# Independent column groups, a new hand-written order, and the rotation's halves exchanged by DMA

## The chip, the cores and the metric

The kernel is one program on one core of a Trainium2 chip. The metric is the time of one execution in device microseconds; three executions of the kernel before took 726.45 to 727.84 us, median 726.69. Five engines work in it beside the DMA engines: TensorE (PE in the profile, its weight loads PEld), VectorE (DVE), ScalarE (ACT), GpSimd (POOL) and SyncE (SP). Each engine runs its own list of instructions in order and waits for the others by semaphores.

## The reference, cut to what matters

Two layers over 256 tokens of width 1024, batch 1, all in float32:

```python
for layer in range(2):
    shift, scale, gate = split(mods[2 * layer], 3)          # mods = silu(c) @ ada_w + ada_b
    h = modulate(x, norm_mix[layer], shift, scale)          # RMS norm, then scale and shift
    if layer == 0:
        y = hgrn2_mixer(h, ...)                             # gated linear recurrence, 8 heads, chunks
    else:
        shared = nsa_shared_kv(modulate(x, kv_norm, ...))   # six projections: k and v, three branches
        y = nsa_mixer(h, ..., shared, cos, sin)             # sparse attention, 16 heads, 4 kv heads
    x = x + gate * y
    h = modulate(x, norm_ffn[layer], *mods[2 * layer + 1][:2])
    x = x + gate2 * swiglu(h, ffn_w_in[layer], ffn_w_out[layer])
```

In the second mixer the keys of two branches and the queries are normalised per head and then rotated:

```python
def apply_rope(x, cos, sin):
    x1, x2 = jnp.split(x, 2, axis=-1)
    return jnp.concatenate([x1 * cs - x2 * sn, x2 * cs + x1 * sn], axis=-1)
```

The attention has a compressed branch (softmax over 15 compressed blocks), a selected and a window branch, whose three outputs are added with sigmoid gates.

## The kernel before, in words

**Products.** Activations lie with channels on the partitions and the 256 tokens along the free dimension. A float32 product is made of three products of float32r numbers: weights and activations are split into a high part (a rounded copy) and a low part (the rest), and high·high, high·low and low·high are summed in PSUM (`mm3`, L531 to L533; `gemm_wide`, L543 and L544, takes high·[high low] in one matmul of 512 columns and low·high in one of 256). The high part of a weight is an ACT copy (L321), the low part a DVE subtraction (L325), two halves of 1024 columns for each 1 MB of weights.

**Weights.** `SCHED` is the list of all 1 MB weight tiles in the order of their use. SP loads them (L298) into a ring of four buffers; `process` splits the next one, or hands it to the code that uses it raw.

**Orders.** A scheduling framework puts the traced instructions in order on each engine: a list by priority, which is the order of tracing, moved by offsets (`PRI`, `first`), with an instruction eligible when those that it depends on are done in the framework's own reckoning. `after` adds an edge between two instructions of one engine. Two matmuls into one PSUM tile count as dependent, whichever partitions they write. The strings in `ORDER` give the order of tracing within the two mixers:

- first mixer (`"hgrn"`): `D`n decays of heads (logs, cumulated products; DVE and ACT), `S`n scores, `V`n values and the squares for their norm, `T`n the end of the values (scale, transpose), `i`n and `g`n products with weight tiles, `G` and `H` gates, `o`n the output product. A token with `+` is put into a generator, `between`; `S1/4` takes four steps of it after each of 12 groups of score matmuls; `x` runs what is left of it. i and g have 16 steps each, T has 2.
- second mixer (`"nsa"`): `q`n product for a quarter of the queries, their squares and rotation; `c` the two halves of the compression with raw weights; `K` the modulated input of the value projections, split; `G` gates; `n`n head norm of the queries of two `q` tokens; `w`n value projections; `x`n compressed softmax; `s`n scores of a pair of heads and their softmax; `v`n transposes and the product with the values; `a` one weight tile of a modulation that TensorE computes.

**Modulations on TensorE** (`ada_pe`, L427): with a left operand of 32 columns the array is used in four column groups. A row of four matmuls, one for each group, accumulates one slice of the input channels into four partition groups of one PSUM tile. s1 and g0 (traced in the first mixer), g2 and s3 (in the second) are of this kind.

**Values** (`attend_values`): for a pair of heads, the probabilities are transposed (ptt, L1561), copied to SBUF (PT; one of four by DVE, three by ACT) and multiplied with the values in two column groups, one for each head of the pair: five steps for each half, into one PSUM tile po (L1578).

**Rotation.** `raw_heads` copies a projection to hu and squares it. `rotate` exchanges the halves of 32 channels by four ACT copies between partition groups (us, L1240; us has two buffers), then DVE makes gain·u·cos (L1243), swap·us·sin (L1244) and their sum (L1245). `head_norm` sums the squares (hs, L1255), takes the inverse root on ACT and DVE, spreads it over the partitions (hb, L1264 and L1265) and multiplies (L1266, for queries also L1268). It is called for the two keys before the string begins, and by `n`.

**End.** `ffn` ends with eight chunks of the output product of 22 weight blocks each. `residual` adds gate times the product to x, for `gemm_wide` in two DVE steps (L796), and SP stores the chunk (L800).

Of the kernel before, what the change touches and what calls it, by code (L numbers as in the profile page):

```python
# [55 lines left out]
def _ada_g(l):  # L56
# [6 lines left out]

ORDER = {
    "hgrn": (
        "D0 k i0 +g0 +i1 +g1 S0/4 x c0 c1 V0 D1 i2 +i3 +g2 +T0 +g3 S1/4 x G0 V1 T1 o0 H o1 G1 o2 o3"
    ).split(),
    "hada": [1, 1, 2, 2, 3, 3, 4, 4, 7, 7, 8, 8],
    "f0": [7, 7, 8, 8, 9, 13, 15, 16, 16, 16, 21, 21, 22, 23, 25, 26, 28, 29, 31, 32],
    "nsa": (  # L70
        "q0 c1 c0 K G q1 n0 x0 w0 s0 q3 s1 q2 w1 s2 v0 v1 n1 s3 a s4 v2 a v3 a x1 s5 a a s6 v4 v6 s7 v5 a v7 a a a a a a"
    ).split(),
    "f1": [15, 16, 24, 29],
}
# [125 lines left out]
class K:  # L200
# [101 lines left out]
    def process(self):  # L302
        nc = self.nc
        n = self.n_proc
        kind, name, i = SCHED[n]
        if SCHED[n] in LATE:
            self.n_proc += 1
            return
        self.issue(n + 1)
        self.n_proc += 1  # L310
        t = self.raw.pop(n)
        if kind in ("lin", "half"):
            ws = []
            for h in range(1 if kind == "half" else 2):
                c = CH // 2
                u = t[:, h * c:h * c + c]
                self.n_half += 1
                pool = self.xp if self.xp is not None and self.n_half % XMOD < 2 else self.wp
                wh = pool.tile([P, c], F32R, tag="wh", name=f"wh{n}_{h}")
                wl = pool.tile([P, c], F32R, tag="wl", name=f"wl{n}_{h}")  # L320
                r = nc.scalar.copy(wh, u)  # L321
                if h and self.hold is not None:
                    self.after(r, self.hold)
                    self.hold = None
                r = nc.vector.tensor_tensor(wl, u, wh.bitcast(F32), op=ALU.subtract)  # L325
                if (name, i, h) in ROOTED:
                    self.after(r, self.last_dg)
                ws.append((wh, wl))
            self.ready.append((name, i, ws))
        elif kind == "raw":  # L330
            self.rawready[(name, i)] = (n, t)
            self.held.add(n)
        elif kind in ("pe_ss", "pe_g"):
            self.ada_pe(kind[3:], name, i, t)
        else:
            self.ada(kind, name, i, t)
        self.issue(n + RAW + 1)
# [78 lines left out]
    def ada_pe(self, kind, l, i, t):  # L416

        nc = self.nc
        ss = kind == "ss"
        q = 512 if ss else 256  # L420
        if i == 0:
            self.aps = self.pp.tile([P, 512], F32, tag="ada", bufs=1, name=f"adaps{kind}{l}")
        ks = [i] if ss else [2 * i, 2 * i + 1]
        last = i == (7 if ss else 3)
        for n, k in enumerate(ks):
            for j in range(4):
                nc.tensor.matmul(self.aps[32 * j:32 * j + 32, :q], lhsT=self.c32[:, k],  # L427
                                 rhs=t[:, n * D + j * q:n * D + (j + 1) * q], start=k == 0, stop=k == KD - 1,
                                 tile_position=(0, 32 * j))
        if not last:  # L430
            return
        m, A, bias = self.ada_tiles(l)
        nb = q // P
        sm = self.tp.tile([P, 512], F32, tag="junk", bufs=1, name="adasm")
        nc.scalar.copy(sm[:, :q], self.aps[:, :q])
        pt = self.pp.tile([P, 4, P], F32, tag="ada", bufs=1, name="adat")
        for b in range(nb):
            nc.tensor.transpose(pt[:, b, :], sm[:, b * P:(b + 1) * P], self.c("ident"))
        lo, hi = (0, 16) if ss else (16, 24)
        nc.vector.tensor_tensor(m[:, lo:hi].rearrange("p (j b) -> p j b", b=nb),  # L440
                                pt.rearrange("p b (j r) -> p j b r", r=32)[:, :, :nb, 0],
                                bias[:, lo:hi].rearrange("p (j b) -> p j b", b=nb), op=ALU.add)
        if ss:
            nc.vector.scalar_tensor_tensor(A, m[:, 8:16], 1.0, self.col(self.gain(l)), op0=ALU.add, op1=ALU.mult)
            self.mods[("A", l)] = A
            self.mods[("shift", l)] = m[:, 0:8]
        else:
            self.mods[("gate", l)] = m[:, 16:24]
# [367 lines left out]
    def hgrn(self):  # L816
# [3 lines left out]
        with self.tc.tile_pool(name="hg", bufs=1) as gp, self.tc.tile_pool(name="hg2", bufs=2) as g2:  # L820
# [112 lines left out]
            for t in ORDER["hgrn"]:  # L933
# [5 lines left out]
                elif t[0] == "S":  # L939
                    As.update(self.hgrn_scores((2 * n, 2 * n + 1), Xs, q3, g2, between, int(t[3:] or 0)))  # L940
                elif t[0] == "+":
                    between = chain(between, {"g": gate_steps, "o": out_steps, "i": value_steps, "T": end_steps}[t[1]](int(t[2])))
                elif t[0] == "x":
                    for _ in between:
                        pass
                elif t[0] == "i":
                    for _ in value_steps(n):
                        pass
                elif t[0] == "g":
                    if n < 2:  # L950
                        nc.scalar.copy(graw[:, n], gate_in(n))
                    else:
                        gin[n] = None
                elif t[0] == "c":
                    nc.scalar.copy(graw[:, n], gin[n])
                elif t[0] == "V":
                    ends[n] = (2 * n, 2 * n + 1), *self.hgrn_values((2 * n, 2 * n + 1), As, v[n], g2, q), g2, q
                elif t[0] == "T":
                    for _ in self.values_end(*ends[n]):
                        pass  # L960
                elif t[0] == "G":
                    gated(n)
                elif t[0] == "H":
                    late.extend(gate_act(m, gin[m], "X") for m in (2, 3))
                elif t[0] == "o":
                    for _ in out_steps(n):
                        pass
            self.end_residual(nxt)
            self.h = nxt

# [198 lines left out]
    def ffn(self, l):  # L1169
        nc = self.nc  # L1170
        with self.tc.tile_pool(name=f"ff{l}", bufs=1) as fp, self.tc.tile_pool(name=f"ft{l}", bufs=2) as tp, \
# [38 lines left out]
            for m in range(KD):  # L1210
# [5 lines left out]
                            tiles[nch * 16 + 8 * h + e] = t  # L1216
                    nch += 1
                ps = self.acc_tile(f"ffo{l}_{m}")
                self.gemm_wide(ps, [tiles.pop(m * NF + k) for k in range(NF)], lambda k: g[:, k])
                self.residual(ps[:, 0], m, gate, nxt, ps[:, 1])  # L1220
            self.end_residual(nxt)
            self.h = nxt

# [10 lines left out]
    def rotate(self, u, gain, swap, kr, name):  # L1234
# [2 lines left out]
        us = self.s2.tile([P, 2, S], F32, tag="us", bufs=2, name=f"us{name}")  # L1237
        for b in range(4):
            d, e = 32 * b, 32 * (b ^ 1)
            nc.scalar.copy(us[d:d + 32], u[e:e + 32])  # L1240
        cs = self.c("cos")[:, None, :].to_broadcast([P, 2, S])
        sn = self.c("sin")[:, None, :].to_broadcast([P, 2, S])
        nc.vector.scalar_tensor_tensor(kr, u, gain, cs, op0=ALU.mult, op1=ALU.mult)  # L1243
        nc.vector.scalar_tensor_tensor(us, us, swap, sn, op0=ALU.mult, op1=ALU.mult)  # L1244
        nc.vector.tensor_tensor(kr, kr, us, op=ALU.add)  # L1245

    def head_norm(self, pairs, kr, gain=None, kn=None):

        nc = self.nc
        ps = self.m_tile([P, S], "hs")  # L1250
# [6 lines left out]
        r = self.rsqrt(ps, [P, S], "hr")  # L1257
        rh, rl = (self.tp.tile([P, S], F32R, tag=f"hr{e}", bufs=1, name=f"hr{e}") for e in "yt")
        self.split(rh, rl, r)
        for i, (u, _) in enumerate(pairs):  # L1260
            pb = self.m_tile([P, 2, S], "hb")
            for m in range(2):
# [7 lines left out]
    def nsa(self):  # L1270
        nc = self.nc
        with self.tc.tile_pool(name="ns", bufs=1) as sp, self.tc.tile_pool(name="ns2", bufs=2) as s2, \
                ExitStack() as self.late:
            self.sp, self.s2 = sp, s2
            self.PC, self.Pt = {}, {}
            self.rsel = sp.tile([P, 4 * P], F32R, name="rsel")
            rsel = s2.tile([P, 2, S], F32, tag="hsq", bufs=2, name="rselr").rearrange("p a b -> p (a b)")
# [16 lines left out]
            with ExitStack() as early:  # L1294
# [20 lines left out]
                hq = self.full_pair(1, 2, xr, s2, QACT)  # L1315
                for br in range(2):
                    self.rotate(kk[br][0], self.col("k_norm", 1 + br), self.col("k_swap", 1 + br), KR[:, :, br], f"k{br}")
                self.head_norm(kk, [KR[:, :, br] for br in range(2)])
                for kind in range(2):
                    self.cmp_blocks(*dk[kind], kind, Dt[kind], sk)  # L1320
                self.QR = sp.tile([P, 8, S], F32, name="QR")
# [20 lines left out]
                for t in ORDER["nsa"]:  # L1342
                    n = int(t[1:] or 0)
                    if t[0] == "q":
                        query(n)
                    elif t[0] == "K":
                        hk.append(self.full_pair(0, "kv", xr, s2, KACT))
                        early.close()
# [201 lines left out]
    def attend_values(self, j):  # L1550
# [20 lines left out]
        for br in range(2):  # L1571
            for e, t in ((0, slice(0, S)), (1, slice(P, S))):
                steps.append((br, self.V[:, e, br, P * g:P * g + P].rearrange("p (h d) -> p h d", h=2),
                              slice(0, S) if e == 0 else slice(S, 384), t))
        for n, (br, w, r, t) in enumerate(steps):
            for half in range(2):
                rhs = r if br is None else PT[half, br][:, r]
                nc.tensor.matmul(po[64 * half:64 * half + 64, t], lhsT=w[:, half], rhs=rhs, start=n == 0,  # L1578
                                 stop=n == len(steps) - 1, tile_position=(0, 64 * half))
        self.split(self.O[0][:, j, :256], self.O[1][:, j, :256], po)  # L1580


# [117 lines left out]
```

## Time and profile before

| | us |
|---|---|
| median of 3 runs | 726.69 |
| the profiled execution | 726.5 |
| its span, first to last instruction | 724.7 |
| TensorE busy | 711.4 |
| VectorE busy | 578.6 |
| ScalarE busy | 433.7 |
| GpSimd busy | 0.4 |

Stages on TensorE, from the timeline: first mixer to about 170 us, first feed-forward to 359, keys and values of the second mixer from 359, its string of tokens from 385 to 510, output product to 537, second feed-forward to the end. The granted clock is 1.00 throughout.

How to read it: the span's 13.3 us without TensorE work lie at the start, at the end and in a few places between. Times in rows are microseconds from the span's start; `xN` is a count of instructions, a float32 matmul counts as two (two passes), a float32r one as one. An arrow `<-` at the end of a row names what the idle time before it waited for. A group row gives busy time, the mean duration in ns, and idle time before it. Matmuls overlap, so what one costs is read from start to start.

### The profile page before, as it was taken

The numbers are of one execution on the slowest core, as the hardware profiler recorded it, in microseconds if no ns is written. First come the engines' busy times: TensorE is split into PE (matmuls) and PEld (weight loads), VectorE is DVE, ScalarE is ACT, GpSimd is POOL, SyncE is SP. The second block draws the span as 40 slices with busy tenths as digits, with TensorE's granted clock in tenths as the row PEclk, the third lists the DMA queues.
The fourth block names the chain that finished last, engine by engine and source line by source line (L and its number), as shares of the span: only waits on it lengthen the run. The fifth ranks groups of instructions, "written<-read, shape, count | busy, mean of one in ns | idle before, by whom it ended". The sixth has DMA issues, their size and how long they took to land.

```text
span 724.7 us, 14519 instructions
## 1 busy us (share of the span) xinstructions
PE 711.4 (98%) x5821; PEld 626.3 (86%) x5821; DVE 578.6 (80%) x1177; ACT 433.7 (60%) x849; POOL 0.4 (0%) x5
## 2 busy tenths in 40 slices
PE   7999999999999999999998999999999999999997
PEld 4998788799999999988897996555999888888886
DVE  6997896589999889889598898677779878776651
ACT  5669877567635454544379776558657656564430
POOL 0000000000000000000000000000000000000000
PEclk9999999999999999999999999999999999999999
DMA  8899865734599889889546631663745757556710
GB/s 354 323 395 359 338 249 187 282 117 175 176 335 378 318 334 345 317 307 339 194 147 232 232 124 52 233 233 123 284 175 175 250 207 256 205 196 231 256 65 23
DMA packets 27158, 172.48 MB, mean 238 GB/s; under 512 B 2897, under 2 KB 4305, under 8 KB 7250
## 3 DMA queue, kind: packets, MB, share of 16 engines
q1 hardware_dynamic: 26656, 170.80, 64.2%
q8 instruction: 46, 0.75, 0.4%
q10 hardware_dynamic: 434, 0.74, 0.3%
q14 instruction: 22, 0.18, 0.1%
HBM read 170.48 MB, written 1.05 MB: 237 GB/s over the span
## 4 chain that ended last, share of the span: by engine, by line
PE 84%; ACT 7%; DVE 6%; DMA 2%; issue 1%; ACTq 0%
PE ffo L543 11%; PE ff L531 6%; PE ff L533 6%; PE ff L532 6%; PE ffo L544 6%; PE ff L543 5%; PE po L1578 3%; PE ff L544 2%; PE adapsss L427 2%; PE ptt L1561 2%; PE s L1521 1%; PE nso L531 1%; ACT wh L321 1%; PE nso L533 1%; PE cmp L1416 1%; PE hg_g L531 1%
## 5 line engine op out<-in xcount | busy, mean ns | idle before, releaser
L321 ACT CAST wh<-raw 128x1024 fp32r<-128x1024 f32 x199 | 206.7, 1048 | 152.2 <-PE ffo L543 47.7
L325 DVE TENSOR_TENSOR wl<-raw,wh 128x1024 fp32r<-128x1024 f32 x199 | 241.3, 1222 | 64.7 <-ACT wh L321 64.4
L543 PE MATMUL ffo<-g,wh 128*128 128x512 f32 x352 | 123.6, 394 | 0.0
L532 PE MATMUL ff<-hl,wh 128*128 128x256 f32 (+1 forms) x352 | 99.2, 282 | 0.0
L544 PE MATMUL ffo<-g,wl 128*128 128x256 f32 x352 | 99.1, 282 | 0.0
L533 PE MATMUL ff<-hh,wl 128*128 128x256 f32 (+1 forms) x352 | 99.1, 282 | 0.0
L531 PE MATMUL ff<-hh,wh 128*128 128x256 f32 (+1 forms) x352 | 99.0, 282 | 0.0
L543 PEld LDWEIGHTS ffo<-g,wh 128*128 128x128 f32 x352 | 66.2, 188 | 15.5
L389 DVE CUSTOM_DVE_ANT_0 junk<-raw,crep 128x1024 f32<-128x1024 f32 x64 | 78.0, 1218 | 0.5 <-DMA raw<-in_w 0.4
L531 PEld LDWEIGHTS ff<-hh,wh 128*128 128x128 f32 x352 | 66.3, 189 | 0.2 <-ACT hh L582 0.2
L533 PEld LDWEIGHTS ff<-hh,wl 128*128 128x128 f32 x352 | 66.5, 189 | 0.0
L532 PEld LDWEIGHTS ff<-hl,wh 128*128 128x128 f32 x352 | 66.4, 189 | 0.0
L544 PEld LDWEIGHTS ffo<-g,wl 128*128 128x128 f32 x352 | 66.1, 188 | 0.0
L543 PE MATMUL ff<-h,wh 128*128 128x512 f32 x152 | 54.1, 394 | 0.0
L544 PE MATMUL ff<-h,wl 128*128 128x256 f32 x152 | 42.6, 281 | 0.0
L543 PEld LDWEIGHTS ff<-h,wh 128*128 128x128 f32 x152 | 28.7, 189 | 6.6
L465 ACT ACTIVATE Pt<-Pt,nm 128x128 f32<-128x128 f32 x64 | 28.2, 443 | 8.5 <-DVE nm L1530 8.4
L796 DVE SCALAR_TENSOR_TENSOR x<-ffo,mod,x 128x256 f32<-128x256 f32 x32 | 15.4, 482 | 20.0 <-PE ffo L544 19.7
L544 PEld LDWEIGHTS ff<-h,wl 128*128 128x128 f32 x152 | 28.7, 189 | 0.0
L526 ACT CAST g<-fg 128x256 fp32r<-128x256 f32 x44 | 17.8, 404 | 17.8 <-DVE fg L1201 16.7
L1526 DVE CUSTOM_DVE_ANT_0 Pt<-s,cst 128x128 f32<-128x128 f32 (+1 forms) x64 | 19.1, 352 | 2.8 <-PE s L1521 2.8
L1037 DVE TENSOR_TENSOR rf<-rf 128x512 f32<-128x512 f32 x28 | 18.5, 692 | 2.2 <-ACT X L1034 1.2
(490 smaller groups left out, 1733.2 us busy)
## 6 DMA issues: line engine op xcount, KB each, us to landing
raw<-in_w SPq DMA_DIRECT2D x153, 1024.0 KB, 5.1
raw<-in_w SPq DMA_DIRECT2D x11, 512.0 KB, 6.6
w1late<-in_w SPq DMA_DIRECT2D x2, 1024.0 KB, 6.1
x<-in_x SPq DMA_DIRECT2D x2, 512.0 KB, 4.9
out<-x SPq DMA_DIRECT2D x8, 128.0 KB, 1.9
cst<-in_cst ACTq DMA_DIRECT2D x1, 558.0 KB
rselr<-in_rsel SPq DMA_DIRECT2D x1, 256.0 KB, 3.7
w<-in_w SPq DMA_DIRECT2D x1, 128.0 KB, 3.6
```

Source lines behind the costliest of these rows:

```text
L321: r = nc.scalar.copy(wh, u)
L325: r = nc.vector.tensor_tensor(wl, u, wh.bitcast(F32), op=ALU.subtract)
L389: r = nc.vector.tensor_tensor_reduce(out=junk, in0=t[:, h * D:(h + 1) * D], in1=self.crep, scale=1.0, scalar=0.0, op0=ALU.mult, op1=ALU.ad ...
L465: r = nc.scalar.activation(out, in_, func, **kw)
L531: mm(ps, lhsT=wh, rhs=hh, start=first, stop=False)
L532: mm(ps, lhsT=wh, rhs=hl, start=False, stop=False)
L533: return mm(ps, lhsT=wl, rhs=hh, start=False, stop=last)
L543: mm(ps, lhsT=w[k][0], rhs=b, start=k == 0, stop=False)
L544: mm(ps[:, 0], lhsT=w[k][1], rhs=b[:, 0], start=False, stop=k == n - 1)
L1037: nc.vector.tensor_tensor(fr, fr, ap(rf, 2 * W, [1, 2], [2, n], [0, b]), op=ALU.mult)
L1526: nc.vector.tensor_tensor_reduce(out=Pt[half][:, br, o:o + n], in0=ps[half][:, br], in1=cs[:, S - n:], scale=1.0, scalar=-3e38, op0=ALU.ad ...
L1578: nc.tensor.matmul(po[64 * half:64 * half + 64, t], lhsT=w[:, half], rhs=rhs, start=n == 0, stop=n == len(steps) - 1, tile_position=(0, 64 ...
```

## The change

- `ORDER["hgrn"]`: `V0` moves from before `D1` to behind `i2 +i3`; `+g3` moves from before `S1/4` to behind it.
- `ORDER["nsa"]`: `K` first; `c0` before `c1`; `w0` before `q1`; a new token `R` behind `q1`, ahead of `n0`; `q3 w1 s0 s1 s2 q2` in place of `s0 q3 s1 q2 w1 s2`; the tokens `a` at other places.
- `ada_pe`: the four matmuls of a row are declared not to depend on each other. `attend_values`: the same for the matmuls of the two halves of po.
- `rotate`: the exchange is made by four DMAs of 32 partitions x 512 numbers (64 KB) from GpSimd's queue; the cosine term stays; sine term and sum move to `rotate_end`, called at the start of the second half of the head norm (`head_mul`), and come behind the last low part traced so far (`last_wl`). For the keys `head_mul` is called at `R`.
- `ffn`, last output chunk of the second layer alone: the product with the low part of g first, into a PSUM tile of its own and added to x; then high·high and low·high in matmuls of 256 columns, added in one step.

```diff
     "hgrn": (
-        "D0 k i0 +g0 +i1 +g1 S0/4 x c0 c1 V0 D1 i2 +i3 +g2 +T0 +g3 S1/4 x G0 V1 T1 o0 H o1 G1 o2 o3"
+        "D0 k i0 +g0 +i1 +g1 S0/4 x c0 c1 D1 i2 +i3 V0 +g2 +T0 S1/4 +g3 x G0 V1 T1 o0 H o1 G1 o2 o3"
...
     "nsa": (
-        "q0 c1 c0 K G q1 n0 x0 w0 s0 q3 s1 q2 w1 s2 v0 v1 n1 s3 a s4 v2 a v3 a x1 s5 a a s6 v4 v6 s7 v5 a v7 a a a a a a"
+        "K q0 c0 c1 G w0 q1 R n0 x0 q3 w1 s0 s1 s2 q2 v0 v1 n1 a s3 a s4 v2 a v3 a x1 s5 s6 v4 v6 s7 a a a a v5 a v7 a a a"
...
@@ process
                 r = nc.vector.tensor_tensor(wl, u, wh.bitcast(F32), op=ALU.subtract)
+                self.last_wl = r
...
@@ ada_pe
         for n, k in enumerate(ks):
+            row = []
             for j in range(4):
-                nc.tensor.matmul(self.aps[32 * j:32 * j + 32, :q], lhsT=self.c32[:, k],
+                row.append(nc.tensor.matmul(self.aps[32 * j:32 * j + 32, :q], lhsT=self.c32[:, k],
...
+                for r in row[:-1]:
+                    self.tc.declare_no_dep(row[-1].ins, r.ins, query=mybir.DependencyQuery.ANY, reason="other partitions")
...
@@ ffn
-                self.gemm_wide(ps, [tiles.pop(m * NF + k) for k in range(NF)], lambda k: g[:, k])
-                self.residual(ps[:, 0], m, gate, nxt, ps[:, 1])
+                ws = [tiles.pop(m * NF + k) for k in range(NF)]
+                if nxt is None and m == KD - 1:
+                    mm, pl = nc.tensor.matmul, self.acc_tile(f"ffo{l}_low")
+                    for k in range(NF):
+                        mm(pl[:, 0], lhsT=ws[k][0], rhs=gl[:, k], start=k == 0, stop=k == NF - 1)
+                    self.residual(pl[:, 0], m, gate, nxt, part=True)
+                    for k in range(NF):
+                        for e in range(2):
+                            mm(ps[:, 0], lhsT=ws[k][e], rhs=gh[:, k], start=k == 0 and not e, stop=k == NF - 1 and e == 1)
+                    self.residual(ps[:, 0], m, gate, nxt)
+                else:
+                    self.gemm_wide(ps, ws, lambda k: g[:, k])
+                    self.residual(ps[:, 0], m, gate, nxt, ps[:, 1])
...
@@ rotate
         for b in range(4):
             d, e = 32 * b, 32 * (b ^ 1)
-            nc.scalar.copy(us[d:d + 32], u[e:e + 32])
+            nc.gpsimd.dma_start(us[d:d + 32], u[e:e + 32])
         cs = self.c("cos")[:, None, :].to_broadcast([P, 2, S])
+        nc.vector.scalar_tensor_tensor(kr, u, gain, cs, op0=ALU.mult, op1=ALU.mult)
+        self.swapped.append((kr, us, swap))
+
+    @first("rot")
+    def rotate_end(self):
+
+        nc = self.nc
         sn = self.c("sin")[:, None, :].to_broadcast([P, 2, S])
-        nc.vector.scalar_tensor_tensor(kr, u, gain, cs, op0=ALU.mult, op1=ALU.mult)
-        nc.vector.scalar_tensor_tensor(us, us, swap, sn, op0=ALU.mult, op1=ALU.mult)
-        nc.vector.tensor_tensor(kr, kr, us, op=ALU.add)
+        for kr, us, swap in self.swapped:
+            r = nc.vector.scalar_tensor_tensor(us, us, swap, sn, op0=ALU.mult, op1=ALU.mult)
+            self.after(r, self.last_wl)
+            nc.vector.tensor_tensor(kr, kr, us, op=ALU.add)
+        self.swapped = []
...
@@ head_norm
+        if later:
+            return rh, rl
+        self.head_mul(rh, rl, pairs, kr, gain, kn)
+
+    def head_mul(self, rh, rl, pairs, kr, gain=None, kn=None):
+
+        nc = self.nc
+        self.rotate_end()
...
@@ nsa
-                self.head_norm(kk, [KR[:, :, br] for br in range(2)])
+                ks = [KR[:, :, br] for br in range(2)]
+                rs = self.head_norm(kk, ks, later=True)
...
+                    elif t[0] == "R":
+                        self.head_mul(*rs, kk, ks)
...
@@ attend_values
+        done = [], []
...
+        for a in done[0]:
+            for b in done[1]:
+                self.tc.declare_no_dep(b.ins, a.ins, query=mybir.DependencyQuery.ANY, reason="other partitions")
+                self.tc.declare_no_dep(a.ins, b.ins, query=mybir.DependencyQuery.ANY, reason="other partitions")
```

More of the change, by code (lines that the diff above doesn't have):

```diff
@@ L425, in ada_pe @@
         for n, k in enumerate(ks):
+            row = []
             for j in range(4):
-                nc.tensor.matmul(self.aps[32 * j:32 * j + 32, :q], lhsT=self.c32[:, k],
-                                 rhs=t[:, n * D + j * q:n * D + (j + 1) * q], start=k == 0, stop=k == KD - 1,
-                                 tile_position=(0, 32 * j))
+                row.append(nc.tensor.matmul(self.aps[32 * j:32 * j + 32, :q], lhsT=self.c32[:, k],
+                                            rhs=t[:, n * D + j * q:n * D + (j + 1) * q], start=k == 0, stop=k == KD - 1,
+                                            tile_position=(0, 32 * j)))
+                for r in row[:-1]:
+                    self.tc.declare_no_dep(row[-1].ins, r.ins, query=mybir.DependencyQuery.ANY, reason="other partitions")
         if not last:
@@ L967, in hgrn @@
                         pass
+            assert next(between, None) is None
             self.end_residual(nxt)
@@ L1239, in rotate, with head_norm @@
             d, e = 32 * b, 32 * (b ^ 1)
-            nc.scalar.copy(us[d:d + 32], u[e:e + 32])
+            nc.gpsimd.dma_start(us[d:d + 32], u[e:e + 32])
         cs = self.c("cos")[:, None, :].to_broadcast([P, 2, S])
-        sn = self.c("sin")[:, None, :].to_broadcast([P, 2, S])
-        nc.vector.scalar_tensor_tensor(kr, u, gain, cs, op0=ALU.mult, op1=ALU.mult)
-        nc.vector.scalar_tensor_tensor(us, us, swap, sn, op0=ALU.mult, op1=ALU.mult)
-        nc.vector.tensor_tensor(kr, kr, us, op=ALU.add)
-    def head_norm(self, pairs, kr, gain=None, kn=None):
+        nc.vector.scalar_tensor_tensor(kr, u, gain, cs, op0=ALU.mult, op1=ALU.mult)
[3 more added lines that the diff above has]
+        nc = self.nc
+        sn = self.c("sin")[:, None, :].to_broadcast([P, 2, S])
+        for kr, us, swap in self.swapped:
[3 more added lines that the diff above has]
+        self.swapped = []
+    def head_norm(self, pairs, kr, gain=None, kn=None, later=False):
         nc = self.nc
@@ L1274, in nsa @@
             self.sp, self.s2 = sp, s2
+            self.swapped = []
             self.PC, self.Pt = {}, {}
@@ L1577, in attend_values @@
                 rhs = r if br is None else PT[half, br][:, r]
-                nc.tensor.matmul(po[64 * half:64 * half + 64, t], lhsT=w[:, half], rhs=rhs, start=n == 0,
-                                 stop=n == len(steps) - 1, tile_position=(0, 64 * half))
+                done[half].append(nc.tensor.matmul(po[64 * half:64 * half + 64, t], lhsT=w[:, half], rhs=rhs, start=n == 0,
+                                                   stop=n == len(steps) - 1, tile_position=(0, 64 * half)))
+        for a in done[0]:
+            for b in done[1]:
+                self.tc.declare_no_dep(b.ins, a.ins, query=mybir.DependencyQuery.ANY, reason="other partitions")
+                self.tc.declare_no_dep(a.ins, b.ins, query=mybir.DependencyQuery.ANY, reason="other partitions")
         self.split(self.O[0][:, j, :256], self.O[1][:, j, :256], po)
```

## The prediction

> **What bounds the kernel now.** I read the page's head first, then TensorE's list of waits, then the busy time by stretches.
>
> ```profile
> span 724.7 us, 14519 instructions
> PE 711.4 (98%) x5821; PEld 626.3 (86%) x5821; DVE 578.6 (80%) x1177; ACT 433.7 (60%) x849; POOL 0.4 (0%) x5
> ...
> PE hs L1255 <- ACT hsqk L1305: 1.0, 1, 1.0
> PE nq L531 <- ACT wh L321: 1.0, 1, 1.0
> ...
> 120.00:140.00 20.00, 19.92 (x348) 14.76 (x346) 10.86 (x25) 10.41 (x17) 0.00 (x0) 1.00 0.87 305
> 385.00:390.00 5.00, 4.00 (x29) 3.33 (x29) 4.55 (x11) 4.54 (x10) 0.00 (x0) 1.00 1.01 421
> 390.00:395.00 5.00, 4.01 (x34) 3.81 (x33) 3.78 (x8) 4.85 (x10) 0.00 (x0) 1.00 0.57 188
> 420.00:425.00 5.00, 5.00 (x45) 5.00 (x44) 5.00 (x11) 3.68 (x8) 0.00 (x0) 1.00 0.41 138
> 440.00:445.00 5.00, 4.57 (x27) 3.06 (x26) 4.13 (x24) 3.61 (x17) 0.00 (x0) 1.00 0.00 0
> ```
>
> TensorE is the bound: idle for 724.7 - 711.4 = 13.3 us only, and two one-microsecond waits in the middle both stand for ACT. So two things can be won: idle time, above all the 2.0 us in 385 to 395, and time in which TensorE counts as busy but works badly. For the second the order of its instructions is read from the timeline:
>
> ```profile
> 130.80 1.90 PE L427 MATMUL adapsss<-raw,c 128*32 128x512 f32 x10
> 132.78 0.65 PE L1163 MATMUL hgt<-cst,o 128*128 128x128 f32 x4
> 133.37 1.06 PE L427 MATMUL adapsss<-raw,c 128*32 128x512 f32 x6
> 134.35 0.39 PE L531 MATMUL hg_g<-h,wh 128*128 128x256 f32 x1
> ...
> 417.03 0.62 PE L427 MATMUL adapsg<-raw,c 128*32 128x256 f32 x2
> 417.58 0.39 PE L985 MATMUL v<-wh,h 128*128 128x256 f32 x1
> ...
> 474.28 1.90 PE L427 MATMUL adapsss<-raw,c 128*32 128x512 f32 x10
> 476.12 1.20 PE L1561 MATMUL ptt<-cst,Pt 128*128 128x128 f32 x9
> ...
> 481.34 1.92 PE L427 MATMUL adapsss<-raw,c 128*32 128x512 f32 x16
> 483.20 0.44 PE L1504 MATMUL pct<-cst,css 128*128 128x128 f32 x2
> ...
> 500.84 1.04 PE L427 MATMUL adapsss<-raw,c 128*32 128x512 f32 x2
> 501.82 0.55 PE L1561 MATMUL ptt<-cst,Pt 128*128 128x128 f32 x3
> ```
>
> The modulation matmuls use a quarter of the columns each (128*32; two passes per matmul), and the four quarters of a row run side by side. A whole pair of rows (x16) holds TensorE from 481.34 to 483.20, 1.86 us. A single quarter (x2) holds it from 500.84 to 501.82, 0.98 us, as long as three quarters (x6, 133.37 to 134.35). A row broken in two so costs about one microsecond more, and the trace has such breaks at 130.80, 417.03, 474.28 (x10, a row and a lone quarter) and 500.84.
>
> **The change, part by part.** The sum is made against the profiled execution (726.5 us, span 724.7); the median of the runs, 726.69, stands 0.2 above it.
>
> *The exchange of channel halves leaves ACT.*
>
> ```profile
> L1240 ACT COPY usk<-huk 32x512 f32<-32x512 f32 x8 | 4.9, 618 | 0.2
> ...
> 387.51 0.62 PE L1255 MATMUL hs<-hsqk,cst 128*32 128x256 f32 x2 [0.99 <-ACT hsqk L1305]
> ...
> 394.90 0.39 PE L531 MATMUL nq<-hh,wh 128*128 128x256 f32 x1 [0.99 <-ACT wh L321]
> ```
>
> Eight copies of 0.618 us for the two keys, four ahead of each of these two waits: 2.5 us of ACT time each, against a wait of 1.0. Both waits should go; what is late next is the square's input from DVE, so I take -2.0 (bounds -2.5, each wait with its restart, and 0). The other 16 copies, 16 x 0.618 = 9.9 us, belong to the queries; ACT is not what TensorE waits for there, so they bring nothing by themselves.
>
> *In their place: 24 DMAs of 64 KB from POOL, and sine terms on DVE later.* No DMA from POOL is in this trace, nor a transfer from the on-chip memory to itself. The nearest transfer is out<-x, 128 KB in 1.9 us:
>
> ```profile
> out<-x SPq DMA_DIRECT2D x8, 128.0 KB, 1.9
> ...
> L1244 DVE SCALAR_TENSOR_TENSOR usq<-usq,cols,cst x4: 746/747/750, 398.8 to 439.6; 128x512 f32<-128x512 f32 x4
> L1245 DVE TENSOR_TENSOR QR<-QR,usq 128x512 f32<-128x512 f32 x4 | 2.7, 684 | 0.0
> L325 DVE TENSOR_TENSOR wl<-raw,wh 128x1024 fp32r<-128x1024 f32 x199 | 241.3, 1222 | 64.7 <-ACT wh L321 64.4
> ```
>
> DVE's work is the same, 0.747 + 0.684 a rotation; only its place moves. For the keys there is all the time from 388 to step R. For the first two queries there is not: us has two buffers, the keys hold both until rotate_end in step R, so query 0's four DMAs start only when the first key's 1.43 us of DVE is done, and its sine term waits on DVE for the landing, with the next weights' splits (1.22 us each) queued behind it. The cover on TensorE is what follows R: half of q1 and the whole of q3 and w1, 48 matmuls each at 0.12 us from start to start (as 720.19 to 720.31 in the rows of the tail): 14.5 us. But DVE also splits the weights of that cover, and in 420 to 425 it is busy 5.00 of 5.00, so a stall there is not free. Bounds: 0 if all is covered; 9.5 if each of the four DMAs takes 1.9 after the other (worked out with the second rival). I take +1.0, nearer the covered end: the four pieces go to one list of engines that 1 MB loads already share, so I expect them side by side. POOL's only other work here, clearing KC, can queue behind a waiting DMA; its reader x0 comes after R, so I cost that at nothing. The DMAs share the 16 engines with SP's weight loads (share 1.01 in 385 to 390): the keys' wait a little, and no one waits for them.
>
> Two rows of DVE bear on whether POOL can issue freely beside it:
>
> ```profile
> L758 DVE TENSOR_SCALAR t<-xr,modA,mod 128x256 f32<-128x256 f32 x4 | 1.5, 408 | 0.0
> L527 DVE TENSOR_TENSOR hl<-t,hh 128x256 fp32r<-128x256 f32 x8 | 3.1, 418 | 0.0
> ```
>
> The one-source form takes 408 ns and the two-source form 418 for the same 256 columns: neither runs at a doubled rate, so I give a lock between the two engines a small chance (third rival). The Trainium skill's page "SBUF — State Buffer", section "SBUF: two separate sides", speaks against the change here: while DVE runs in a two-port mode, GpSimd cannot write descriptors and its DMA stands still; no run here shows it so far, and the rows show no such mode. By the Trainium skill's page "DMA: Bandwidth & Descriptors", section "Anatomy of one DMA — SWDGE (gpsimd) path", one such DMA would take about 2.0 us + 64 KB / 436 GB/s = 2.15 us, an estimate from that page; the sum by it would be the same.
>
> *Quarters and halves declared independent.* For the modulation rows: s1 takes 132.78 - 130.80 + 134.35 - 133.37 = 2.96 for two rows against 1.86 whole, so 1.1; the gate's lone quarter at 417.03 costs 0.55; in s3 the lone quarter at 500.84 and the one at the end of 474.28 cost about 1.0 each. Together -3.7 if all go, 0 if the list that orders the instructions still breaks rows when something more urgent comes. I take -1.9. For po:
>
> ```profile
> 450.00:512.00 62.00, 19.82 (x160) 11.31 (x158) 3.01 (x8) 2.86 (x8) 1.00 0.55 199
> ...
> 478.72 1.56 PE L1578 MATMUL po<-PT,V 128*64 128x256 f32 x16
> 480.21 1.20 PE L1561 MATMUL ptt<-cst,Pt 128*128 128x128 f32 x9
> ...
> 504.54 0.43 PE L1578 MATMUL po<-PT,V 128*64 128x128 f32 x2
> 504.90 1.06 PE L427 MATMUL adapsss<-raw,c 128*32 128x512 f32 x6
> ```
>
> 16 well-paired ones (half of them 256 wide, half 128) take 1.49 us, so a 256 takes 0.124 and the four of PC 0.50; eight times 1.99 is 15.9 against 19.82: -3.9 at best. But free halves may also run ahead alone, since half 1's weights come through ACT and half 0's first through DVE; a lone step (0.36 us at 504.54) for each of eight gives +2.9. Between, I take -0.5.
>
> *The tail.*
>
> ```profile
> 720.19 0.28 PE L544 MATMUL ffo<-g,wl 128*128 128x256 f32 x1
> 720.31 0.39 PE L543 MATMUL ffo<-g,wh 128*128 128x512 f32 x1
> 720.54 0.28 PE L544 MATMUL ffo<-g,wl 128*128 128x256 f32 x1
> 720.86 1.00 DVE L796 SCALAR_TENSOR_TENSOR x<-ffo,mod,x 128x256 f32<-128x256 f32 x2 [6.67 <-PE ffo L544]
> 721.89 0.33 SPq L800 DMA_DIRECT2D out<-x  x1
> ```
>
> The last output chunk ends in two dependent DVE steps, 1.00 us; one of them now runs under the matmuls: -0.5. The wide step (512 columns, 0.23 from start to start) becomes two of 256 (0.12 each): 22 x 0.01, +0.1 with rounding. Sum -0.4, bounds -0.5 and +0.1. DVE's work before these steps ended 6.67 us earlier, so the weights are split in time for the reversed use.
>
> *The orders.* In the first mixer V0 goes behind D1 and i2, and g3's 16 steps are no longer placed by hand inside S1 (34 steps are left for 48 places). TensorE is 0.08 us idle in 120 to 140, so there is little to win; V0's squares on ACT now stand behind D1's copies, and T0 waits for them: 0, bounds ±1.5. In the second, K stands first but writes the buffer that holds the late weights until c1 has run, so its splits begin after c1 with the gate and q1 as cover on TensorE: 0, up to +3 if that cover is late. s0 is put behind q3 and w1, which should take some of the 0.43 us idle in 440 to 445: -0.3, bounds ±1.0.
>
> Sum: -2.0 + 1.0 - 1.9 - 0.5 - 0.4 + 0 + 0 - 0.3 = -4.1; 726.5 - 4.1 = 722.4, and with the 0.2 of the median 722.6.
>
> **The rivals.** *Freed orders do not regroup* (the declaration doesn't do what it says, or lone halves run ahead): -1.9 and -0.5 become 0 and +1.2, so 726.7 - 2.0 + 1.0 + 1.2 - 0.4 - 0.3 = 726.2, no change. For it: the breaks stand where a more urgent instruction came in. Against: so far each quarter is ordered behind the one before it, and whatever is ready can slip between.
>
> *The exchange is late* (slower): POOL's four DMAs land one after the other at 1.9 us, 7.6 a query. At R DVE then stands 7.6 - 1.4 = 6.2 us at query 0's sine term and as long at query 1's, 12.4 in all, with the splits of the cover behind it; TensorE has split weights for half a query, 2.9 us, and then waits 9.5. In place of the +1.0: 726.7 - 5.1 + 9.5 = 731.1. For it: us has only two buffers. Against it: the DMA engines' share in 420 to 425 is 0.41, so there is room for them side by side. It turns the sign from 5.1 us of TensorE's wait on, and is measurably slower from 6.6.
>
> *DVE locks POOL out:* by that mechanism each of four DMAs waits for one long DVE step, 1.22 us, 4.9 a query; DVE stands 4.9 - 1.4 = 3.5 at three sine terms that have a step R or n1 close behind, 10.5 less 2.9: 726.7 - 5.1 + 7.6 = 729.2.
>
> *All regroups:* rows, halves, and a wait of 0: 726.7 - 2.5 - 3.7 - 3.9 - 0.5 - 0.3 = 715.8. Against it: the lone quarters are where the list filled a gap, and gaps stay.
>
> **How the numbers follow.** The forecast, 722.6 (its own range 719.0 to 725.0, half of each term's way to its bounds or a little less), 0.51; freed orders that do not regroup 0.18; late exchange 0.14; lock 0.03; all regroups 0.14. A difference under 0.2% (1.45 us) can't be told from none, as the runs shown lie 726.45 to 727.84. Faster 0.51 + 0.14 = 0.65, same 0.18, slower 0.17. The range takes in nearly all of the full regrouping and the lock, and leaves out the late exchange at full price: 716.0 to 729.5, under 0.2 left out.
>
> **What would show it.** The waits of hs for hsqk and nq for wh in 385 to 395 gone, TensorE's idle time there near 0; L427 rows only as x8, x16 or x32; po's busy time under 19; one L796 step after the last matmul. Against it: DVE idle at the line of the sine terms with a DMA named as releaser, lone po halves, a wait of v or nq for the splits of weights, and TensorE idle between c1 and w0.

## The result and the profile after

| | before | after |
|---|---|---|
| median of six runs, us | 726.57 (726.22 to 727.84) | 721.16 (720.36 to 723.27) |
| profiled execution / its span, us | 726.5 / 724.7 | 723.27 / 721.5 |

The ratio is 0.9927, 95% interval 0.9912 to 0.9942: 5.3 us faster (4.2 to 6.4). The forecast was 722.6. The profiled execution of the changed kernel was the slowest of its six, 2.1 us above their median; most of the reason turns up in its trace below.

The head of its page, with the rows of its DMA part for the new transfers and the weights:

```profile
span 721.5 us, 14615 instructions
...
PE 710.4 (98%) x5843; PEld 628.2 (87%) x5843; DVE 578.9 (80%) x1177; ACT 418.5 (58%) x825; POOL 12.3 (2%) x29
...
w1late<-in_w SPq DMA_DIRECT2D x2, 1024.0 KB, 8.7
...
usq<-huq POOLq DMA_DIRECT2D x16, 64.0 KB, 2.9
...
usk<-huk POOLq DMA_DIRECT2D x8, 64.0 KB, 5.8
```

ACT lost its 24 copies (433.7 to 418.5 us), POOL got 24 issues of 0.5 us. TensorE is still the bound. Its three longest waits inside the second mixer (line, what it waited for, us in all, times, longest):

```profile
PE v L990 <- DVE h L531: 1.0, 1, 1.0
PE v L988 <- ACT h L530: 0.4, 1, 0.4
PE hs L1280 <- ACT hsqk L1339: 0.3, 1, 0.3
```

Of the two waits of 1.0 for ACT, that of hs is down to 0.3 and that of nq is gone; a wait of the first value projection (w0), 1.4 in two parts, is new. What it waits for, h, is not a weight but w0's input, the activations that `K` modulates and splits (high part on ACT, low part on DVE). This idle time is called the hole at w0 below. The same by stretches (TensorE, weight loads, DVE, ACT, POOL, granted clock, DMA share, GB/s):

```profile
385.00:390.00 5.00, 4.72 (x37) 4.11 (x36) 4.94 (x12) 4.63 (x9) 1.96 (x4) 1.00 1.01 367
390.00:395.00 5.00, 5.00 (x47) 4.61 (x47) 3.66 (x6) 1.51 (x4) 0.00 (x0) 1.00 1.02 351
420.00:425.00 5.00, 5.00 (x47) 4.46 (x46) 4.78 (x9) 3.42 (x8) 1.12 (x3) 1.00 0.66 236
440.00:445.00 5.00, 4.94 (x19) 2.39 (x18) 5.00 (x37) 2.37 (x11) 0.00 (x0) 1.00 0.01 3
400.00:405.00 5.00, 4.26 (x23) 4.26 (x24) 4.93 (x12) 2.74 (x8) 0.00 (x0) 0.66 0.63 267
```

In 385 to 395 TensorE is idle for 0.28 us instead of 1.99. But in 400 to 405 it is idle for 0.74, does only 23 matmuls where a full stretch holds some 45, and the granted clock is 0.66 on the average. The rows of the modulation and the end, from the timeline:

```profile
482.09 1.05 PE L429 MATMUL adapsss<-raw,c 128*32 128x512 f32 x4
...
495.91 1.06 PE L429 MATMUL adapsss<-raw,c 128*32 128x512 f32 x6
...
718.05 0.48 DVE L800 SCALAR_TENSOR_TENSOR x<-ffo,mod,x 128x256 f32<-128x256 f32 x1 [4.70 <-PE ffo L1232]
```

Rows of four are still broken (x4 is two quarters, x6 three), though each quarter was declared independent; and one DVE step of 0.48 is left after the last matmul, where there were two of 1.00 together.

The main measure below is TensorE's time for one tile in 380 to 545, in which matmuls that overlap count once. First adapsss before, po before, then both after:

```profile
380.00:545.00 165.00, 9.98 (x64) 1.00 0.50 186
380.00:545.00 165.00, 20.14 (x160) 1.00 0.50 186
```

```profile
380.00:545.00 165.00, 10.19 (x64) 0.99 0.56 201
380.00:545.00 165.00, 18.17 (x160) 0.99 0.56 201
```

The modulation rows cost as much as before; po costs 1.97 us less.

### The profile page after: what moved, and what is told of

The parts are those of the page before. It is cut to its first block, busy times and chain, and to the rows that moved or that the text cites. A ratio compares the mean times of both kernels' runs of the same rounds, so it can differ in the third digit from the quotient of the medians.

```text
span 721.5 us, 14615 instructions
## 1 busy us (share of the span) xinstructions
PE 710.4 (98%) x5843; PEld 628.2 (87%) x5843; DVE 578.9 (80%) x1177; ACT 418.5 (58%) x825; POOL 12.3 (2%) x29
## 4 chain that ended last, share of the span: by engine, by line
PE 80%; DVE 7%; ACT 6%; DMA 4%; issue 2%; SPq 0%; ACTq 0%; DVEq 0%
PE ffo L547 11%; PE ff L535 7%; PE ff L537 7%; PE ff L536 6%; PE ffo L548 5%; PE ff L547 5%; DMA raw<-in_w 3%; PE ff L548 2%; PE po L1616 2%; PE adapsss L429 2%; DVE wl L325 2%; ACT wh L321 2%; PE ptt L1598 2%; PE s L1558 2%; ACT Pt L469 1%
## 5 line engine op out<-in xcount | busy, mean ns | idle before, releaser
L547 PE MATMUL ffo<-g,wh 128*128 128x512 f32 x330 | 116.0, 394 | 0.0
L548 PE MATMUL ffo<-g,wl 128*128 128x256 f32 x330 | 93.0, 282 | 0.0
L547 PEld LDWEIGHTS ffo<-g,wh 128*128 128x128 f32 x330 | 62.0, 188 | 14.5
L548 PEld LDWEIGHTS ffo<-g,wl 128*128 128x128 f32 x330 | 62.0, 188 | 0.0
```

The costliest lines, as they stand in the source:

```text
L547: mm(ps, lhsT=w[k][0], rhs=b, start=k == 0, stop=False)
L548: mm(ps[:, 0], lhsT=w[k][1], rhs=b[:, 0], start=False, stop=k == n - 1)
```

## The experiments

Each is timed in five rounds against the kernel before, whose medians lay between 726.28 and 726.89.

**The declarations taken out.**

```diff
-                for r in row[:-1]:
+                for r in []:
...
-        for a in done[0]:
+        for a in []:
```

> The kernel after, with both declarations of independence left out. The built instruction lists of all five engines, waits included, come out the same as with them. Theory A (the declarations do nothing, the gain has other causes): the time of the kernel after, 721.2 us within 0.7, and by the profile again rows of the modulation broken in the same places (a lone quarter near 131 and near 447). Rival B (they regroup the column groups, as the forecast had it, -2.4 us): 723 to 724 us. It also gives a second profile of the same program: if the hole of 398 to 404 us, where TensorE waits for the value projection's input and the granted clock falls, belongs to the program and not to one run, it is there again.

Measured: 722.33 us, ratio 0.9945 (0.9933 to 0.9957), span of the profiled run 720.2. The instruction lists of all five engines, waits included, are the same with and without the declarations but for two neighbouring matmuls of po, which change places (first steps in the second half of two pairs): for this framework, in this place, the declarations regrouped nothing. Why, isn't known. So this is also a second look at the changed kernel, and two things follow. The two medians of what is all but one program differ by 1.2 us (5.3 and 4.0 us below the kernel before), and smaller differences between variants mean nothing. And in its trace the hole at w0 is there without the low clock:

```profile
395.00:400.00 5.00, 4.67 (x40) 1.00 1.02 406
400.00:405.00 5.00, 4.15 (x35) 1.00 0.68 287
```

Idle for 1.18 us against 1.43 in 395 to 405 of the other trace, yet 75 matmuls against 59. The profiled execution of the changed kernel was long partly because there the clock fell behind the hole: from nq's first matmul to nso's last it took 149.5 us, this one 147.8, the kernel before 151.1.

**q1 ahead of w0.**

```diff
-        "K q0 c0 c1 G w0 q1 R n0 ...
+        "K q0 c0 c1 G q1 w0 R n0 ...
```

> The kernel after with q1 ahead of w0 in the second mixer's order, all else the same. Theory A (w0 put ahead of q1 leaves TensorE without cover while K is split behind c1: idle 1.4 us and a lowered clock for some 5 us, about 3 us in all): 718 to 719.5 us, no wait of v for h, clock 1.00 from 395 to 415. Rival B (the hole is made by the late landing of weight tiles, whatever their order, 5.8 us of ACT's wait for a tile): 721 us within 0.7, the hole stands in front of q1 instead.

Measured: 723.44, ratio 0.9962 (0.9950 to 0.9975); the hoped-for gain didn't come. The wait of w0 is gone, since q1 covers K's splits, and TensorE, which takes its list in order, then waits for the compressed keys' chain instead; po went to 19.43:

```profile
PE hidt L1468 <- DVE hid L1460: 1.6, 1, 1.6
```

Against the second timing of the change, 722.33, the loss is 1.1 us, within what two timings of one program differ by.

**Rows and halves kept together by priority.**

```diff
+                with self.tc.high_priority(offset=20000 if j else 0):
...
+                with self.tc.high_priority(offset=20000 if half else 0):
```

> The kernel after with rows of four and pairs of two held together: no declarations, but the second to fourth matmul of a modulation's row and the second half's matmul of po get a high priority, so that they follow the first at once. Theory A (a broken row costs about 1 us each, as the trace's rows show): modulation of s1, g2 and s3 takes 2.9 us less, po 1.3 less, time 717 to 719. Rival B (rows break because something more urgent is ready, so whole rows delay the softmax chain by as much): 721 us within 0.7, with longer waits of ptt and s.

Measured: 726.86, ratio 1.0003 (0.9992 to 1.0013): all of the gain is lost. The rows did get cheap, 8.32 us for adapsss where the changed kernel takes 10.19. But the modulation's matmuls were finished by 486 us, and then TensorE had nothing to put between the softmax steps (TensorE alone; clock, DMA share):

```profile
490.00:495.00 5.00, 1.60 (x9) 0.96 0.58 208
495.00:500.00 5.00, 4.76 (x25) 0.70 0.00 0
500.00:505.00 5.00, 3.98 (x36) 1.00 0.55 210
```

3.40 us in the first of these stretches are one wait, of adat (the transposes that close the modulation) for adasm on ACT, which stood behind the softmax's exponentials. Idle time in 380 to 545 rose from 2.2 (the trace without declarations) to 7.5, more than the 1.9 of adapsss and 0.4 of the gate's rows. A broken row is dear by itself and a cheap filler in its place.

**The exchange back on ACT, all else as changed.**

```diff
-            nc.gpsimd.dma_start(us[d:d + 32], u[e:e + 32])
+            nc.scalar.copy(us[d:d + 32], u[e:e + 32])
```

> The kernel after with the exchange of halves made by four ACT copies again in place of the four DMAs; order, step R and the late sine terms stay. Theory A (the exchange off ACT pays in 385 to 395, 1.7 us of TensorE's idle time): 722.5 to 724 us, and the waits of hs for hsqk or of nq for wh are back. Rival B (the order alone gives the gain; the DMAs take as much from the weight loads, which run at share 1.0 there): 721 us or less.

Measured: 734.3, ratio 1.0113 (1.0100 to 1.0126), some 13 us slower than the change and far more than any theory gave. One part of theory A came true: the wait of hs is back, and TensorE is idle for 1.63 us in 385 to 395, where the change has 0.28 and the kernel before 1.99.

```profile
PE hs L1280 <- ACT hsqk L1339: 1.0, 1, 1.0
```

So the exchange's place is what makes this wait come and go, but most of the 13 us is elsewhere. The list scheduler reckons with ACT's copies and put TensorE's list in another order, with lone quarters late in the mixer, two more of them at 511.39 and 514.19:

```profile
501.59 1.05 PE L429 MATMUL adapsss<-raw,c 128*32 128x512 f32 x2
507.48 1.04 PE L429 MATMUL adapsss<-raw,c 128*32 128x512 f32 x2
509.03 1.05 PE L429 MATMUL adapsss<-raw,c 128*32 128x512 f32 x2
```

Its adapsss and po by the main measure:

```profile
380.00:545.00 165.00, 14.34 (x64) 1.00 0.50 181
380.00:545.00 165.00, 21.75 (x160) 1.00 0.50 181
```

Against the changed kernel's trace adapsss costs 4.15 more, the gate's rows 0.6, po 3.58, and 2.2 are idle time: 10.5 of the 10.8 between the spans. (Against the second trace, which has no low clock, the same four terms make 10.8 of 12.1.) A lone quarter takes a microsecond, as four do.

**Is it the order, or ACT?** To tell these apart, a kernel that keeps the exchange on DMA, but whose rows and halves the scheduler cuts up almost as it did with the copies on ACT (G is moved ahead of c0):

```diff
-        "K q0 c0 c1 G w0 q1 R n0 ...
+        "K q0 G c0 c1 w0 q1 R n0 ...
```

> The changed kernel with the gate put before c0 (K q0 G c0 c1 w0 q1 R): the exchange stays on DMA, but the list scheduler cuts the modulation rows and the halves of po into nearly the same single pieces as it did with the copies on ACT. Theory A (what the copies on ACT cost was the cutting: adapsss +4.2, adapsg +0.6, po +3.6 us of TensorE, and only 2.4 us were idle time): 728 to 731, adapsss 13.5 to 14.5 us and po 21 to 22 us in 380 to 520. Theory B (the copies cost by ACT's time on the path, and the cutting is a by-product): 720 to 724.

Measured: 736.1, ratio 1.0127 (1.0113 to 1.0142), even above the expected 728 to 731. Its adapsss and po:

```profile
380.00:545.00 165.00, 14.34 (x64) 0.98 0.51 185
380.00:545.00 165.00, 22.37 (x160) 0.98 0.51 185
```

All of TensorE in two later stretches:

```profile
405.00:410.00 5.00, 5.00 (x34) 0.73 0.60 233
...
415.00:420.00 5.00, 5.00 (x33) 0.71 0.16 28
```

adapsss costs the same 14.34, without a copy on ACT. So most of what the copies cost in this order was the cutting. The surplus over the expected time is mostly two waits of w0 for its input h (3.0 us) and two stretches of low clock behind them. The second of these waits leads back to the exchange: DVE stands for query 0's halves, whose four pieces took a median of 6.0 us to land beside the weight loads, and K's split comes behind it on DVE.

```profile
411.35 0.75 DVE L1267 SCALAR_TENSOR_TENSOR usq<-usq,cols,cst 128x512 f32<-128x512 f32 x1 [3.43 <-DMA usq<-huq]
412.14 0.69 DVE L1269 TENSOR_TENSOR QR<-QR,usq 128x512 f32<-128x512 f32 x1
412.75 0.75 DVE L531 TENSOR_TENSOR h<-t,h 128x256 fp32r<-128x256 f32 x2
...
413.22 0.39 PE L990 MATMUL v<-wh,h 128*128 128x256 f32 x1 [1.73 <-DVE h L531]
```

**The first mixer and the tail alone, the second mixer as before.**

```diff
     "hgrn": (
-        ... c0 c1 V0 D1 i2 +i3 +g2 +T0 +g3 S1/4 x ...
+        ... c0 c1 D1 i2 +i3 V0 +g2 +T0 S1/4 +g3 x ...
...
@@ ffn
+                if nxt is None and m == KD - 1:
...
```

> The kernel before with only the first mixer's new order and the new tail; the second mixer keeps its old order and its copies on ACT. Theory A (the first mixer brings about 0.7 us, counted from the first matmul, the tail 0.4, and all else lies in the second mixer): 725.4, between 724.9 and 725.9, with the two ACT waits in 385 to 395 and po's busy time of 20.1 us in 380 to 520 as before. Theory B (the start of hgo 1.4 us earlier in the trace is all the first mixer's, the tail gives 0.5): 724.7 or less.

Measured: 724.16 against 726.89, ratio 0.9964 (0.9951 to 0.9977): 2.6 us (1.7 to 3.6), more than theory A gave, and half of the whole gain or more. The second mixer's rows repeat those of the kernel before (adapsss 9.98, po 20.14, both waits of 1.0). Apart, in two more kernels, the first with the `ffn` part of that diff alone, the second with the `hgrn` part alone:

> The kernel before with the new tail alone; both mixers keep their old order. Theory A (one of two dependent DVE steps of 0.5 us after the last matmul goes, nothing else moves): 0.4 to 0.5 below the kernel before, about 725.9. Theory B (the tail carries most of the 2.7 us that the first mixer's order and the tail brought together): 724.6 or less.

> The kernel before with the first mixer's new order alone; the tail and the second mixer are the old ones. Theory A (g3's steps are no longer spread between S1's rows, and hg_g's busy time in 120 to 173 falls from 14.0 to 13.0 us): 1.0 to 1.6 below the kernel before, 724.7 to 725.4. Theory B (the order is worth nothing, as predicted): within 0.4 of the kernel before.

Measured: the tail alone 726.25, ratio 0.9997 (0.9988 to 1.0006), which can't be told from nothing and holds the 0.5 us of its trace; the first mixer's order alone 724.80, ratio 0.9973 (0.9963 to 0.9984), 2.0 us (1.2 to 2.7). hg_g and hg_i in 60 to 147.3, first before, then with the new order:

```profile
60.00:147.30 87.30, 28.09 (x192) 1.00 0.73 269
60.00:147.30 87.30, 26.08 (x192) 1.00 0.73 269
```

```profile
60.00:147.30 87.30, 27.03 (x192) 1.00 0.75 274
60.00:147.30 87.30, 25.63 (x192) 1.00 0.75 274
```

The two products cost 1.5 us less, and they run in fewer pieces between other matmuls: hg_g in 15 where it had 19, hg_i in 11 where it had 13. Which of the order's two moves does it, V0's or g3's, isn't measured apart. From hg_i's first matmul to hgo's first it takes 83.9 us before and 82.2 with the new order (82.2 to 82.7 in four traces that have it). In the kernel with the tail alone, whose first mixer is the old one, it took 84.9, and this wait is in its trace and in none of the others:

```profile
PE hgt L1163 <- DVE o L1160: 1.1, 1, 1.1
```

**The exchange by DMA in the old order,** with the keys' sine terms computed at once; the first mixer and the tail stay as changed.

```diff
+        "R q0 c1 c0 K G q1 n0 x0 w0 s0 q3 ...     (the old string behind R)
```

> The changed kernel with the second mixer's old order, step R put first: the exchange goes by DMA, and the keys' sine terms are computed at once. Theory A (the exchange alone takes out the ACT waits, about 1 us of TensorE's idle time, and the rest of the second mixer's gain comes from how the modulation rows and po happen to be cut into pieces): adapsss here is cut as 1,3,1,4,6,6,1,3,7 from the sixth piece on, no better than before, po into 13 pieces for 16: 723 to 725. Theory B (the exchange by DMA is what brings the gain, whatever the order): 720.5 to 722. Theory C (the keys' sine terms at once make DVE stand for the landing beside 1 MB loads): 727 or more, DVE waiting for a DMA at the sine terms.

Measured: 729.42, ratio 1.0038 (1.0023 to 1.0052), slower than before, as theory C had it. DVE's waits:

```profile
DVE usq L1267 <- DMA usq<-huq: 2.6, 2, 1.7
DVE usk L1267 <- DMA usk<-huk: 2.2, 2, 2.0
```

Here 4.8 us of landing lie bare on DVE, against 0.4 in the changed kernel; TensorE is idle for 6.3 us in 380 to 545, and adapsss costs 12.19 by its cutting. The wait of hs is 0.3 here too, but the DMA in place of the copies is no gain in this order; what the new one has and this one lacks is the distance between issue and sine term. Distance and cutting changed together here, so how the loss divides between them isn't measured apart.

**Three openings of the second mixer.**

```diff
-        "K q0 c0 c1 G w0 q1 R n0 ...
+        "K q0 G c0 c1 q1 w0 R n0 ...     (gate first, q1 before w0)
+        "q0 c1 c0 K G w0 q1 R n0 ...     (K after c0)
+        "K G q0 c0 c1 q1 w0 R n0 ...     (gate second)
```

> The changed kernel with K q0 G c0 c1 q1 w0 R: the gate's matmuls ahead of c0, the second query ahead of w0. By the list, adapsss has seven pieces from the sixth on for eight, adapsg its last 31 in one, po 13 for 14. Theory A (time follows the pieces and the hole between c1 and w0, which q1 now covers): 718.5 to 720.5, faster than the change as it stands. Theory B (as when q1 was put before w0 alone, the hole only moves and the softmax chain gets later): 722 to 724.

Measured: 731.6, ratio 1.0066 (1.0052 to 1.0079). Theory A falls: adapsss costs only 9.15, but TensorE is idle for 11.2 us:

```profile
PE gt L1512 <- ACT gu L1509: 2.8, 1, 2.8
PE po L1616 <- DVE cf L1580: 2.6, 1, 2.6
PE v L990 <- DVE h L531: 1.8, 1, 1.8
```

> The changed kernel with the second mixer's opening in the old order (q0 c1 c0 K G, then w0 q1 R): K's loads are no longer brought forward into the stretch in which the keys' halves travel. Theory A (the hole at 398 to 404 comes from too many loads at once: a 1 MB load takes 7.2 us there against 4.8 before): the 1.2 us of idle time there and the dip of the granted clock are gone, po and adapsg cost 0.6 and 0.4 more for one and two more pieces: 719.5 to 721.5. Theory B (standing first, K is what lets the two ACT waits go and keeps the softmax chain early): 723 to 726.

Measured: 723.89, ratio 0.9963 (0.9950 to 0.9976). The time is that of theory B, but not its reason: the two ACT waits stay gone (hs 0.3). Theory A falls too, since K's place in the string doesn't make the hole: ACT's first split of h starts 0.8 us after the last matmul of the compression in the change's trace and 0.7 here (398.67 and 398.62), w0 starts at 399.1 in both and waits 1.3 us here too, and the 1 MB loads still take 7.1 us. (That c1 stands before c0 in this string makes no difference: the code takes the two halves in turn and doesn't read the digit.) What it costs is a later DMA for the queries (2.0 us of DVE's waiting), 0.8 of hb for ACT, and po 19.24.

> The changed kernel with K G q0 c0 c1 q1 w0 R: modulation rows and po are cut nearly as in the change (adapsss 1,4,4,4,8,2,6,3, po 14 pieces), only the opening differs. Theory A (what the opening costs is the wait for w0's splits, and the gate and q1 ahead of w0 cover it): 719.5 to 721. Theory B (the gate ahead of c0 makes TensorE wait later for the gate's and the compressed keys' chains on DVE and ACT, as in the run with the gate ahead of c0 and c1): 726 to 730, with 3 us of waits or more between 395 and 415.

Measured: 724.07, ratio 0.9968 (0.9955 to 0.9980), between the two theories. The cutting is that of the change (adapsss 10.19, po 18.16), TensorE's idle time 3.7 for 2.2 to 2.5; w0 waits 1.8 us for h, at 408.7 to 410.5 now, and the clock falls behind it (0.69 in 410 to 415). Here the exchange was late: its pieces for query 0 took a median of 6.9 us to land, DVE stood 2.47 us at their sine term, and the split of h that w0 waits for came behind it. With the gate first DVE stood 1.91 us for a query's pieces and w0 waited 1.78 behind it.

No variant came out below the change. Those with q1 ahead of w0, with K after c0 and with the gate second lie only 1.1 to 1.7 us above the second timing of the change, so that they are slower isn't certain.

## Why the prediction was right, and where it wasn't

The sum came out 1.4 us above the measured time, but only because terms that were too small and terms that were too large offset each other; that it came so near is in good part luck.

- *Two ACT waits, -2.0:* idle time in 385 to 395 fell by 1.7. Held.
- *The exchange, +1.0, and the rival "exchange late":* DVE waited 0.4 us for a landing, and no wait of TensorE traces back to it: about 0. The rival fell because the four pieces land side by side and the sine term comes late enough in this order. Its mechanism is real: in the three kernels with the gate ahead of c0 DVE stood 1.9 to 3.4 us for a query's landing with a split of K behind it, and TensorE then waited 1.7 to 1.8. From issue to landing, the four pieces of query 0, then the eight of the keys:

```profile
DMA to landing us min/median/max: 1.9/1.9/2.0
DMA to landing us min/median/max: 5.3/5.8/6.5
```

  The estimate drawn from the Trainium skill's page "DMA: Bandwidth & Descriptors", section "Anatomy of one DMA — SWDGE (gpsimd) path", was 2.15 us; the trace agrees where the DMA engines have room (1.9, at a share of 0.33 in 414 to 417), and not where the weights hold them at a share of 1.0 (5.8).
- *Rows regrouped by the declarations, -1.9:* this step failed. The declarations regrouped nothing, as the run without them shows; s1, g2 and s3 together cost what they did (23.4 us before and after). The rival "freed orders do not regroup" was right about the mechanism and wrong about the time, since the rest of the sum came out larger.
- *po, -0.5:* mis-sized, -1.97, and not through the declarations (18.17 without them too): in the new order it runs in 14 pieces for 16.
- *First mixer, 0, bounds ±1.5:* mis-sized, -2.0. I looked for idle time and found 0.08 us; the gain lay in busy time, hg_i and hg_g in fewer pieces, which I had read for the modulation rows and not for these.
- *K first, 0, up to +3 if the cover is late:* the price came, 1.2 to 1.4 us of waiting, and in the way that the term names: K's splits begin only after the compression's last matmul, and TensorE waits for them. What the term had wrong is the cover. It counted the gate and q1, but the new string puts w0 ahead of q1, so that little more than the gate is left. With K after c0 the wait is the same; with q1 ahead of w0 alone it is gone, and another chain is late. Where the clock falls behind the hole, 1.7 us more are lost.
- *s0 later, -0.3:* idle time in 440 to 445 fell from 0.43 to 0.06. *Tail, -0.4:* 0.5 in the trace, -0.2 (-0.9 to +0.4) by its own runs.
- *DVE locks POOL out:* no sign of it. POOL's issues took 496 ns throughout the queries, with DVE busy 4.78 of 5.00 in 420 to 425.

Measured apart, the first mixer and the tail bring 2.6 us; the second mixer has the rest of the 5.3. In the trace without the low clock it takes 3.3 us less than before (147.8 for 151.1), of which its idle time in 380 to 545, 2.2 for 3.3, and po, 2.0 less, account for 3.0: 1.7 of ACT waits are won and 1.2 lost again at w0.

## What to carry to other kernels

Where TensorE is 98% busy, count in how many pieces its long products run, at each place that an order touches: in the two kernels with the most pieces here, lone column groups and resumed products cost 8.3 and 9.0 us more than in the change, added idle time 2.2 and 2.1. Where a scheduler orders the list, removing work from one engine can reorder another's, so compare the lists, not only the times, before you put a gain down to the engine that was relieved. And a filler that is made cheap and early is missing later: look at what fills the gaps before you tidy it away.

## What was unexpected of the hardware

The low clock has one size. Over stretches of 5 us it reads 0.66 to 0.75, but in steps of 1 us it is half the clock for 3.4 us, with full clock before and after. In the changed kernel (TensorE; clock, DMA share, GB/s):

```profile
401.00:402.00 1.00, 1.00 (x7) 0.53 1.01 426
402.00:403.00 1.00, 1.00 (x6) 0.50 0.86 360
403.00:404.00 1.00, 1.00 (x6) 0.50 0.25 107
404.00:405.00 1.00, 1.00 (x9) 0.76 0.06 25
```

Half the clock for 3.4 us costs 1.7 us of work, and where two traces can be compared the second mixer took just 1.7 us longer with the dip. The other dips in the traces kept here have the same size: one each with rows kept together, the old order, the gate first and the gate second, two with the rows in pieces. Each stands behind 1.3 to 3.4 us in which TensorE had been idle. But it doesn't come behind every such hole: not behind 1.65 us in 405 to 410 with q1 ahead of w0, not behind 2.79 us before 401.28 with the gate first, and not behind the hole at w0 in the second trace of the change. What decides it isn't settled.

The dips also explain part of the scatter. Of the 67 runs of the kernel before that were timed beside the experiments, the 14 with a mean clock of 0.997 or 0.998 have a median of 727.9 us, the other 53 one of 726.3.
